# First norm's modulation weights from the second quarter on: halves in working tiles, with priorities that fall by quarter

## The chip, the cores and the metric

The kernel runs on one core of one Trainium2 chip. The metric is the device time of one execution in microseconds (us): the median of several runs, smaller is better. Beside it stands one profiled execution, from which every row of a view below is taken. TensorE (PE) multiplies matrices, VectorE (DVE), ScalarE (ACT) and GpSimd (POOL) work elementwise, SyncE (SP) issues the DMA transfers. Each engine works through its own instructions in a fixed order and waits where an operand or a buffer isn't ready.

## The reference

Four transformer layers in a row on one sequence of 256 tokens (plus 256 context tokens in the first one), 1024 channels, all in float32. Every norm of every layer is modulated by vectors that are computed from a conditioning vector `c`; this is the part that the change touches. Cut to what matters:

```python
# first_block, layer 0 (even mixer) and layer 1 (odd mixer)
ml = split(silu(c)     @ ada_w[layer] + ada_b[layer], 6)   # 1024 -> 6*1024, for the 256 latent tokens
mc = split(silu(c_ctx) @ ada_w[layer] + ada_b[layer], 6)   # the same for the 256 context tokens
a_lat = rms_norm(h_lat, norm1_w) * (1 + ml[1]) + ml[0]
a_ctx = rms_norm(h_ctx, norm1_w) * (1 + mc[1]) + mc[0]
o_lat, o_ctx = mixer(a_lat, a_ctx, ...)                    # layer 0: a_lat @ w_in (1024 x 2240), attention + GLA
h_lat = h_lat + ml[2] * o_lat
h_lat = h_lat + ml[5] * mlp(rms_norm(h_lat, norm2_w) * (1 + ml[4]) + ml[3])
# second_block, two hybrid layers of the same form on the result, with weights w_mod (1024 -> 6*1024) and SwiGLU
```

The modulation weights of one layer are 1024 x 6144 float32, 25 MB, used for one or two vectors only.

## The kernel before, in words

**Planning.** The program first records all its operations in program order, without issuing them. A planner then simulates the five engines with a list of costs and writes out the order of each engine by hand. Among the operations that are ready and whose tiles have a free slot, an engine takes the one with the smallest key `(index - early) * 200 - path`, where the index is the operation's place in program order, `early` is a bonus in places that the code sets, and `path` is the planner's cost in ns from there to the end. The SP queue of transfers is ordered in the same way; a load goes out as soon as SP is free, its tile's slot is free, and nothing with a smaller key can go. A transfer that was recorded while `nc.behind` was set isn't issued before the operation of that index. The order written out is fixed: on the chip an engine waits for the operation that is next in it.

**Tiles.** A tag has a fixed number of slots: raw mixer weights `wraw` 4 of 128 x 1024 (512 KB), their split high and low parts `whi`, `wlo` 3 each, raw modulation weights `mraw` 4 of 512 KB (`MODRAW`), working tiles of 128 x 512 (tag `t512`) 47 (`H2`), PSUM banks `ps` 6 and one for the modulation banks (`modps`). Each weight piece is split into a high and a low part (`whi` on ACT or DVE, `wlo` on DVE), and a block of a product is three matmuls: `xnh` with `whi`, `xnh` with `wlo`, `xnl` with `whi`.

**The start of layer 0.** `layer0` needs scale (j = 1) and shift (j = 0) of the first norm. Their weights are stored by quarters: quarter q of j holds the 256 output channels 256q to 256q+255, and its 1 MB is two pieces (h = 0, 1) of 512 KB, one for each half of the input channels. `mod_quarter` loads the two pieces into two `mraw` tiles, multiplies them on PE into one PSUM bank `modq` (16 matmuls that are recorded with `nc.together()`, so that they stay in one run), copies the bank out (`modqs`), transposes it (`modqt`) and adds the bias (two DVE operations on `mod`). After the two vectors of a quarter, `a1` is ready for channel blocks 2q and 2q+1; with it and `rstd`, `norm_mod` makes `ny` and its parts `xnh`, `xnl` of these two blocks. All quarters are recorded with `early` = `EARLYQ` - q * `STEPQ`, with 1500 and 0, so 1500 for all. After quarter 0 (`BEHIND` = 0), `nc.behind` is set to the last load recorded so far, so everything loaded later goes behind quarter 0.

**Around it.** Program order: `x` (eight loads of 256 KB, 2 KB per partition) at indices 14 to 21, the quarters at 36 to 95, the norm's square sums (`sq`, `ss`, `rstd`) and `ny` up to 155, the 18 pieces of the first projection (`ein`) between 156 and 690, the modulation bank of j = 2 (8 pieces through `mod_bank`, `early` 1500) at 1539, those of j = 4, 3, 5 from 1795 on, also with 1500. Each group of `ein` needs all eight blocks of `xnh`, `xnl`; with three pieces split and six PSUM banks, several groups can be partly summed before the last blocks are there. Where PE would sit idle for long, the planner puts dummy matmuls (`filled`), which keep its clock up and compute nothing that is used.

Of the kernel before, what the change touches and what calls it, by code (L numbers as in the profile page):

```python
# [11 lines left out]
F32 = mybir.dt.float32  # L12
# [742 lines left out]
class Kernel:  # L755
    RAW, HI, MODRAW, MODRUN = 4, 3, 4, 2
    LEAD = (5, 2, 1)
    EARLYQ, STEPQ, BEHIND = 1500, 0, 0
    CV, CQ = range(6), ()
    PINP = range(4)  # L760
    EARLY = (1500, 1000, 500, 300)
# [114 lines left out]
    def mod_quarter(self, j, q, dest, bias):  # L876

        nc = self.nc
        ps = self.ps("modq")
        nc.early = self.EARLYQ - q * self.STEPQ  # L880
        raws = [nc.tile(self.mp, [128, 1024], F32, "mraw", "mraw", self.MODRAW) for _ in range(2)]
        for h in range(2):
            nc.sync.dma_start(raws[h], self.A["mod0"][j * 8 + q * 2 + h])
        with nc.together():
            for k in range(4):
                for g in range(4):
                    h, t = g // 2, g % 2
                    self.mm(ps[32 * g:32 * g + 32, 0:128], self.cst[:, 0, h * 4 + k, :],
                            raws[h][:, k * 256 + t * 128:k * 256 + t * 128 + 128], k == 0, k == 3)
        sb = self.t([128, 128], "modqs")  # L890
        nc.scalar.activation(sb, ps[:, 0:128], AF.Copy)
        pt = self.ps("modqt")
        nc.tensor.transpose(pt[:, 0:128], sb, self.c_ident)
        c = slice(j * 8 + q * 2, j * 8 + q * 2 + 2)
        src = pt[:, 0:128].rearrange("p (h t r) -> p h t r", h=2, t=2)
        nc.vector.tensor_tensor(dest[:, c, :], src[:, 0, :, 0:2], bias[:, c].unsqueeze(2).to_broadcast([128, 2, 2]), op=ALU.add)
        nc.vector.tensor_tensor(dest[:, c, :], src[:, 1, :, 0:2], dest[:, c, :], op=ALU.add)
        nc.early = 0
# [1293 lines left out]
```

## Time and profile before

| | |
|---|---|
| median of 3 runs | 1997.41 us (1995.1 to 2007.69) |
| the profiled execution's own time | 1992.15 us |
| its span, first to last instruction | 1990.4 us |
| PE busy | 1915.1 us, 96% of the span |
| DVE, ACT, POOL busy | 1375.8, 891.7, 220.0 us |
| bytes moved | 328.14 MB, mean 165 GB/s |
| mean granted TensorE clock | 0.989 |

PE is busy nearly all the time, but "busy" holds dummy matmuls and matmuls whose modelled ends overlap. What a change at the start is worth is read from the first 62 us: how much of PE's time there is work that is used, and what the rest waits for.

### The profile page before, as it was taken

To read this page: it belongs to the slowest core of one execution; us is meant where nothing else is said; L and a number is where in the kernel's file an instruction comes from. 1 tells how busy PE (TensorE), PEld (TensorE's weight loads), DVE (VectorE), ACT (ScalarE), POOL (GpSimd) and SP (SyncE) were. 2 spreads that over 40 slices of the span, in tenths; PEclk is the share of its full clock that TensorE was granted. 3 is DMA by queue.
4 is the path that set the end of the run, shared out by engine and by line. 5 is a ranking of instruction groups with operands and counts; after the bars stand their busy time and mean duration, and the time that the engine had idled before them with its cause. 6 is when DMAs were issued, how large, how long until landed. Compare 5 with 4: busy or idle time off the path is not lost.

```text
span 1990.4 us, 37698 instructions
## 1 busy us (share of the span) xinstructions
PE 1915.1 (96%) x15067; PEld 1611.4 (81%) x15067; DVE 1375.8 (69%) x2934; ACT 891.7 (45%) x1880; POOL 220.0 (11%) x214
## 2 busy tenths in 40 slices
PE   7999999999999999889999999999999999989998
PEld 5766657888888877677899997877999978679998
DVE  5436777555546468875678777898877689878773
ACT  4125464321212165533355336675654265656541
POOL 1001002000000042013011003200300031012000
PEclk9998999999999999989999999999999999999999
DMA  9683306242323237577437556455555765445651
GB/s 335 211 290 117 117 12 204 62 130 90 118 74 115 77 123 191 181 215 222 127 107 237 187 194 223 155 188 193 177 181 185 250 211 181 148 160 170 184 196 56
DMA packets 108444, 328.14 MB, mean 165 GB/s; under 512 B 27211, under 2 KB 28491, under 8 KB 108140
## 3 DMA queue, kind: packets, MB, share of 16 engines
q1 hardware_dynamic: 108268, 325.73, 50.7%
q8 instruction: 118, 1.93, 0.4%
q14 instruction: 58, 0.48, 0.1%
HBM read 320.45 MB, written 5.24 MB: 164 GB/s over the span
## 4 chain that ended last, share of the span: by engine, by line
PE 80%; DVE 8%; DMA 7%; ACT 3%; issue 2%; POOL 0%; SPq 0%; DVEq 0%; ACTq 0%; POOLq 0%
PE ps L708 62%; PE modps L708 3%; DMA mraw<-in_mod_dram 2%; DMA wraw<-in_hin_dram 2%; PE filled L708 1%; PE sc L708 1%; DVE wlo L708 1%; PE ss L708 1%; DMA wraw<-in_hout_dram 1%; DMA wraw<-in_oin_dram 1%; DVE dlo L708 1%; DVE invt L708 1%; DVE inv L708 1%; PE gdno L708 1%; PE po L708 1%
## 5 line engine op out<-in xcount | busy, mean ns | idle before, releaser
L708 ACT ACTIVATE dhi<-wraw 128x512 fp32r<-128x512 f32 x397 | 237.7, 624 | 264.0 <-PE ps L708 132.4
L708 DVE TENSOR_TENSOR dlo<-wraw,dhi 128x512 fp32r<-128x512 f32 x456 | 305.5, 697 | 69.3 <-PE ps L708 53.6
L708 PE MATMUL ps<-xnh,dhi 128*128 128x256 f32 (+1 forms) x920 | 248.2, 304 | 3.9 <-ACT xnh L708 2.4
L708 PE MATMUL ps<-xnh,dlo 128*128 128x256 f32 (+1 forms) x920 | 248.8, 305 | 1.1 <-DVE dlo L708 1.1
L708 PE MATMUL ps<-xnl,dhi 128*128 128x256 f32 (+1 forms) x920 | 248.3, 304 | 0.1
L708 PE MATMUL ps<-xnh,whi 128*128 128x256 f32 (+1 forms) x776 | 232.6, 331 | 9.8 <-DVE ogg L708 5.7
L708 DVE TENSOR_TENSOR wlo<-wraw,whi 128x512 fp32r<-128x512 f32 x340 | 232.4, 711 | 13.1 <-ACT whi L708 9.2
L708 PE MATMUL ps<-xnh,wlo 128*128 128x256 f32 (+1 forms) x776 | 231.9, 331 | 3.2 <-DVE wlo L708 3.2
L708 PE MATMUL ps<-xnl,whi 128*128 128x256 f32 (+1 forms) x776 | 231.8, 331 | 0.8 <-DVE xnl L708 0.8
L708 PEld LDWEIGHTS ps<-xnh,dhi 128*128 128x128 f32 x920 | 165.4, 191 | 13.5 <-ACT xnh L708 2.9
L708 PEld LDWEIGHTS ps<-xnh,dlo 128*128 128x128 f32 x920 | 165.4, 191 | 10.4 <-DVE dlo L708 1.8
L708 PEld LDWEIGHTS ps<-xnl,dhi 128*128 128x128 f32 x920 | 165.5, 191 | 8.0 <-DVE xnl L708 0.7
L708 DVE CAST whi<-wraw 128x1024 fp32r<-128x1024 f32 x82 | 56.8, 693 | 158.4 <-PE ps L708 133.8
L708 PEld LDWEIGHTS ps<-xnh,whi 128*128 128x128 f32 x776 | 143.7, 193 | 27.7 <-issue 6.2
L708 PEld LDWEIGHTS ps<-xnh,wlo 128*128 128x128 f32 x776 | 144.1, 193 | 21.3 <-DVE wlo L708 4.8
L708 PEld LDWEIGHTS ps<-xnl,whi 128*128 128x128 f32 x776 | 143.7, 193 | 17.1 <-issue 4.6
L708 ACT ACTIVATE whi<-wraw 128x1024 fp32r<-128x1024 f32 x88 | 92.9, 1056 | 102.2 <-PE ps L708 58.4
L708 PE MATMUL ps<-mh,dhi 128*128 128x512 f32 (+1 forms) x336 | 105.9, 336 | 0.1
L708 PE MATMUL ps<-mh,dlo 128*128 128x512 f32 (+1 forms) x336 | 105.9, 336 | 0.0
L708 PE MATMUL ps<-ml,dhi 128*128 128x512 f32 (+1 forms) x336 | 105.8, 336 | 0.0
L708 PE MATMUL modps<-mraw,cst 128*32 128x256 f32 x1408 | 97.7, 393 | 5.8 <-DMA mraw<-in_mod_dram 4.9
L708 POOL TENSOR_TENSOR ny<-x,rstd 128x256 f32<-128x256 f32 (+1 forms) x45 | 50.1, 1140 | 414.8 <-ACT rstd L708 414.8
(558 smaller groups left out, 4114.4 us busy)
## 6 DMA issues: line engine op xcount, KB each, us to landing
mraw<-in_mod_dram SPq DMA_DIRECT2D x192, 512.0 KB
wraw<-in_mlp_dram SPq DMA_DIRECT2D x128, 512.0 KB
wraw<-in_gu_dram SPq DMA_DIRECT2D x88, 512.0 KB
wraw<-in_hin_dram SPq DMA_DIRECT2D x54, 512.0 KB
wraw<-in_dn_dram SPq DMA_DIRECT2D x44, 512.0 KB
wraw<-in_oin_dram SPq DMA_DIRECT2D x25, 512.0 KB
wraw<-in_ein_dram SPq DMA_DIRECT2D x18, 512.0 KB
wraw<-in_hout_dram SPq DMA_DIRECT2D x16, 512.0 KB
```

The costliest lines, as they stand in the source:

```text
L708: getattr(self.real[op.eng], method)(*a, **kw)
```

## The change

Three edits. `STEPQ` becomes 750, so `early` is 1500, 750, 0 and -750 for quarters 0 to 3. The pieces of quarters 1 to 3 no longer go into `mraw` tiles: each 512 KB piece is loaded by two transfers of 256 KB into two working tiles of 128 x 512 named `mrawq` (2 KB per partition and transfer in place of 4 KB). The matmuls are the same, and read the half that holds their columns. Quarter 0 stays as it was. The 12 loads of quarters 1 to 3 become 24, and the operations behind them move up by 12 in program order.

```diff
-    EARLYQ, STEPQ, BEHIND = 1500, 0, 0
+    EARLYQ, STEPQ, BEHIND = 1500, 750, 0
...
         nc.early = self.EARLYQ - q * self.STEPQ
-        raws = [nc.tile(self.mp, [128, 1024], F32, "mraw", "mraw", self.MODRAW) for _ in range(2)]
+        raws = []
         for h in range(2):
-            nc.sync.dma_start(raws[h], self.A["mod0"][j * 8 + q * 2 + h])
+            w = self.A["mod0"][j * 8 + q * 2 + h]
+            if q < 1:
+                raw = nc.tile(self.mp, [128, 1024], F32, "mraw", "mraw", self.MODRAW)
+                nc.sync.dma_start(raw, w)
+                raws.append([raw[:, 0:512], raw[:, 512:1024]])
+            else:
+
+                raws.append([self.t([128, 512], "mrawq") for _ in range(2)])
+                for c in range(2):
+                    nc.sync.dma_start(raws[h][c], w[:, c * 512:c * 512 + 512])
         with nc.together():
...
-                            raws[h][:, k * 256 + t * 128:k * 256 + t * 128 + 128], k == 0, k == 3)
+                            raws[h][k // 2][:, k % 2 * 256 + t * 128:k % 2 * 256 + t * 128 + 128], k == 0, k == 3)
```

## Rows read from the trace of the kernel before

**Rows 1.** The page's head and the busy time of each engine

```profile
span 1990.4 us, 37698 instructions
...
PE 1915.1 (96%) x15067; PEld 1611.4 (81%) x15067; DVE 1375.8 (69%) x2934; ACT 891.7 (45%) x1880; POOL 220.0 (11%) x214
```

**Rows 2.** Windows: length, busy by engine (x instructions), granted clock, DMA share, GB/s

```profile
0.00:27.70 27.70, 16.40 (x118) 10.56 (x118) 16.53 (x40) 15.39 (x27) 2.66 (x6) 1.00 0.94 351
27.70:51.94 24.24, 22.47 (x243) 15.89 (x244) 13.78 (x29) 10.06 (x22) 5.66 (x4) 1.00 0.88 316
51.94:62.04 10.10, 9.90 (x74) 5.29 (x73) 6.84 (x14) 3.16 (x6) 0.00 (x0) 1.00 0.90 322
62.04:127.90 65.86, 65.86 (x390) 48.38 (x389) 23.88 (x41) 10.14 (x18) 0.00 (x0) 1.00 0.66 231
```

**Rows 3.** The same windows for the dummy matmuls alone (PE, PEld)

```profile
27.70:51.94 24.24, 1.56 (x5) 0.86 (x5) 1.00 0.88 316
```

**Rows 4.** Windows by the transfers' stages, columns as in Rows 2

```profile
0.00:15.00 15.00, 7.36 (x72) 5.15 (x73) 3.91 (x12) 5.87 (x12) 0.20 (x4) 1.00 0.87 308
9.00:15.00 6.00, 4.62 (x36) 3.39 (x37) 2.50 (x6) 3.65 (x7) 0.00 (x0) 1.00 1.03 366
15.00:35.00 20.00, 15.88 (x105) 10.69 (x104) 19.79 (x38) 14.06 (x25) 8.12 (x5) 1.00 1.03 403
35.00:40.00 5.00, 5.00 (x78) 3.62 (x76) 1.18 (x4) 0.52 (x2) 0.00 (x0) 1.00 0.55 172
```

**Rows 5.** Waits of SP's queue in 0 to 62: total us, times, longest

```profile
SPq L708 <- PE modq L708: 14.2, 6, 3.1
```

**Rows 6.** Timeline of SP: start, length, transfer, count

```profile
3.07 1.02 SPq L708 DMA_DIRECT2D x<-in_xT_dram  x2
...
7.59 3.74 SPq L708 DMA_DIRECT2D x<-in_xT_dram  x4
...
37.58 0.80 SPq L708 DMA_DIRECT2D mraw<-in_mod_dram  x2
```

**Rows 7.** Timeline of PE, its weight loads and DVE around the first norm

```profile
19.23 2.08 PE L708 MATMUL ss<-sq,cst 128*128 128x512 f32 x2 [2.75 <-DVE sq L708]
...
27.73 0.98 PE L708 MATMUL ps<-xnh,whi 128*128 128x512 f32 x3 [0.94 <-ACT xnh L708]
...
29.44 0.81 PEld L708 LDWEIGHTS modq<-mraw,cst 128*32 128x32 f32 x32 [0.36 <-issue]
29.45 1.08 PE L708 MATMUL modq<-mraw,cst 128*32 128x128 f32 x32
...
46.31 1.08 PE L708 MATMUL modq<-mraw,cst 128*32 128x128 f32 x32
...
51.25 0.69 DVE L708 TENSOR_TENSOR xnl<-ny,xnh 128x512 fp32r<-128x512 f32 x1
```

**Rows 8.** Timeline of ACT around the first norm

```profile
14.46 2.72 ACT L708 ACTIVATE sq<-x 128x512 f32<-128x512 f32 x4 [0.41 <-DMA x<-in_xT_dram]
...
20.76 1.04 ACT L708 ACTIVATE whi<-wraw 128x1024 fp32r<-128x1024 f32 x1
...
24.54 0.63 ACT L708 ACTIVATE rstd<-rstd 128x512 f32<-128x512 f32 x1
```

**Rows 9.** The chain that ended last, in order of time

```profile
62.04 31.77 PE ps L708 x140
...
127.91 7.54 DMA mraw<-in_mod_dram
```

**Rows 10.** Timeline: first instruction of each hybrid layer (ACT), last addition (DVE)

```profile
1216.91 1.31 ACT L708 ACTIVATE lead<-x,ha 128x256 fp32r<-128x256 f32 x3 [0.55 <-DVE x L708]
...
1597.23 0.91 ACT L708 ACTIVATE lead<-x,ha 128x256 fp32r<-128x256 f32 x2 [1.28 <-DVE x L708]
...
1986.72 0.75 DVE L708 TENSOR_TENSOR x<-x,fy 128x256 f32<-128x256 f32 x2
```

**Rows 11.** A window with a lower granted clock, columns as in Rows 2

```profile
160.00:180.00 20.00, 20.00 (x84) 12.13 (x82) 10.75 (x14) 12.84 (x25) 3.35 (x3) 0.74 0.32 105
```

## The prediction

> **What bounds the kernel now.** I read the page's head first [rows 1]: PE is busy for 96% of the span, so a gain has to come from PE time that isn't used, and it is worth what PE can then do earlier. The change touches only the first norm, so I cut the start into windows [rows 2]. From 62.04 to 127.9 PE is busy for 65.86 of 65.86 us: from there on it has work in hand, and whatever the start saves up to 62.04 is carried on. Before the first used projection matmul (27.73 [rows 7]) PE does almost nothing that counts. Between 27.73 and 62.04, that is in 34.3 us, it idles 24.24 - 22.47 = 1.8 and 10.10 - 9.90 = 0.2 us, and 1.6 us are dummy matmuls [rows 2, 3]. So 30.8 us of it are real work. This is the first thing to see: the wait for the last quarters is mostly covered already, by partly summed projection groups.
>
> Next the transfers [rows 4]: 403 GB/s from 15 to 35 us, then only 172 between 35 and 40. SP's waits say why [rows 5]: 14.2 us in which the next load was held because its tile still waited for a modq run on PE. The two loads at 37.58 [rows 6], in the middle of the dip, are of this kind: the modq run that frees their tiles stands in PE's fixed order behind projection matmuls. The last modq run starts at 46.31 and the last block of xnl ends at 51.94 [rows 7].
>
> **The change, part by part.**
>
> *Order of the transfers.* By the keys, quarter 1 (bonus 750) now goes ahead of x, cst, pos and vec (bonus 0, about 40 places earlier); quarter 2 (bonus 0) follows them; quarter 3 (-750) comes behind everything that is recorded within some 750 places behind it and has a free slot. That is not much: four ein pieces (wraw has 4 slots) and four tiles of the j = 2 bank (mraw has 4, free after quarter 0). SP needs about 0.5 us per issue [rows 6], far less than the transfer takes, so in the plan all slots are taken before the first comes free, and quarter 3 is next. In MB, from the shapes: quarter 0 2.10, quarter 1 2.10, x and small constants 2.88, quarter 2 2.10, gup and the first ein piece 0.59, mraw 2.10, three ein pieces 1.57, cst1 0.26, quarter 3 2.10: 15.8 in all. None of these has to wait for a slot on the chip, so SP's 14.2 us of waiting go, and the 12 additional issues (12 x 0.5 = 6 us of SP) lie beside the transfers; without that cover they would cost up to 6 us.
>
> *When they land.* The window to 15 us moved 15 x 308 = 4.62 MB, after that 403 GB/s. Rate of the halves: the nearest rows are the stretch from 9 to 15, mostly x, whose loads have the same shape (366), and 403. Quarter 2 ends at 9.2 MB: 15 + 4.6/0.403 = 26.3 us. Quarter 3 ends at 15.8 MB: 15 + 11.2/0.403 = 42.7; with 6.3 MB at 366 it is 1.6 us later, 44.3. I take 43. Its two modq runs cost PE 2 x (1.08 + 0.36) = 2.9 us [rows 7], and the last xnl ends 5.6 us after the start of the last run, as now (51.94 - 46.31): about 50, and 2 earlier if PE takes the runs at once. So the last blocks come 2 to 4 us earlier.
>
> *What moves off the PE path.* Three modq runs (the second of quarter 1, both of quarter 2) can now run before the first projection matmul, where PE has only dummies: 3 x 1.44 = 4.3 us, with their transposes about 5.3. Matmuls, copies and additions are the same in number, shape and cost.
>
> *What it costs.* x lands 2.10/0.386 = 5.4 us later, at 20.5 us instead of about 15 (0.386 is between the two rates above). Now the last square ends at 17.2 and rstd at 25.17 [rows 8]: 8.0 us, of which only an addition, the ss matmuls (2.08) and two activations (0.63 each) follow from each other, about 4. So rstd is at 25.2 to 29.1, against 25.17, and the first projection matmul, 2.56 us behind it, at 27.8 to 31.7. The first ein piece lands at 27.8 (9.8 MB) and needs 1.04 us for its high part [rows 8] and some 0.7 for the first half of the low one: 29.5. I take 30, so 2.3 us later than now.
>
> *Sum.* Real work left from 30 on: 30.8 - 5.3 = 25.5 us. Idle and dummies: between 0 and today's 3.5, and I take 2, as the supply is close: until xnl is complete three split pieces give 54 matmuls of 31.77/140 = 0.227 us [rows 9], 12.3 us, plus two bank runs and two modq runs of 1.44 us, 18 us for the 18 to 20 us between 30 and 48 to 50. So the state of 62.04 is reached at 30 + 25.5 + 2 = 57.5: **4.5 us** saved, with bounds of 1.3 (31.7 and 3.5) and 8.7 (27.8 and 0). The profiled execution's own time is 1992.15; by this it becomes 1987.6. It lies 5.3 us below the median of the runs, so I take the saving off the median: 1997.4 - 4.5 = 1992.9. The clock doesn't enter: it is granted in full in all windows up to 127.9 [rows 2].
>
> *A rule that speaks against it.* The eight loads of x, of the same shape as the halves, moved at 366 GB/s, 9% below the larger pieces [rows 4], which is the 1.6 us above. The Trainium skill, DMA: Bandwidth & Descriptors (Rules for kernel authors), asks for at least 1 MiB per DMA for full bandwidth, and fits 2.0 us plus bytes over 436 GB/s to one DMA of another issuing path; if each DMA paid that by itself, 24 halves would be an estimated 24 x 2.6 = 62 us where 12 pieces are 12 x 3.2 = 38, so 24 us would be lost. The trace doesn't agree for transfers in a queue: 512 KB pieces reach 403 GB/s, far above what that fit gives one of them.
>
> **The rivals.**
>
> *A. Given back (or never had).* The chain waits for a bank tile at 127.91, 7.54 us long [rows 9]. If the banks of j = 4, 3, 5 land no earlier than now, PE arrives there 4.5 us earlier and waits. Or rstd takes its 8 us and the start gives up what the quarters bring. Against: PE is fully busy up to that point, and the j = 2 bank's first tiles now go out before quarter 3, so the banks are ahead too. Time: 1997.4.
>
> *B. Quarter 3 starves: slower.* Its bonus of -750 puts it behind all four banks by key. If in the plan the mraw tiles come free before SP gets to quarter 3, further tiles pass it: 2.10 MB for each set of four, 5.2 us. The first set is covered by the supply above; from the second on PE runs dry. All of them are 14.7 MB, 36.5 us; less the 14 bank runs that PE does in that time (14 x 1.44 = 20) and 3 of slack, 13 us lost: 2010. Against: tiles come free only when transfers land, and SP is by then long past.
>
> *C. Halves are slow.* The four x loads at 7.59 took 3.74 us, 0.94 each [rows 6], because SP waited for landings. At that pace, not 0.65 (256 KB at 403 GB/s), 24 halves cost 7 us: 1997.4 - 4.5 + 7 = 2000. Against: the whole stretch around these loads moved 366 GB/s. By the estimate from the Trainium skill above (DMA: Bandwidth & Descriptors) it would be some 2017; I leave that inside this rival's chance.
>
> *D. Another order downstream.* The planner's order of everything later shifts. The two hybrid layers run the same program in different orders: 1597.23 - 1216.91 = 380.3 and 1986.72 + 0.75 - 1597.23 = 390.2 us [rows 10], so order alone is worth up to 10 us a layer. A stretch at clock 0.74 for 20 us [rows 11] is worth 20 x 0.26 = 5 us more or less. Time: 1983 or 2003.
>
> **How the numbers follow.** Forecast (a saving of 1.3 to 8.7): 0.60, the time 1992.9. A 0.17, B 0.06, C 0.05, D 0.12, half each way. The range reaches 10 + 5 us (D's two terms) on either side of the forecast and a little more below for its upper bound of 8.7: 1977 to 2007; it holds A, C and most of D, and leaves out B and the tails. A change of 1%, 20 us, is about what a measurement of this kernel can tell from none, as its three runs lie 12.6 us apart. Faster by over 1% would take the forecast and a lucky order in more than one layer, 0.06; slower by over 1% needs B at its worst with an unlucky order, 0.05; within it 0.89.
>
> **What would show it.** Right: SP's waits for PE modq nearly gone in the first 62 us; the DMA near 400 GB/s up to about 43 us without the dip at 35 to 40; x after quarter 1, with the square sums ending some 4 us later; four modq runs of quarters 1 and 2 before the first projection matmul at 29 to 31; the last modq run at 43 to 45; the projection matmuls and bank runs that are done at 62.04 now, done at about 57.5. Wrong: the last modq run behind 52 (B), mrawq transfers below 300 GB/s (C), a longer chain wait near 125 (A), or equal starts and a difference that grows from 300 us on (D).

## The result and the profile after

The changed kernel takes 2004.39 us (median of 20 runs, 1995.25 to 2018.53) against 1993.18 for 20 runs of the kernel before beside it: ratio 1.0059, 95% interval 1.004 to 1.0078. It is slower by 0.6%, 11 to 12 us, where 4.5 us less were forecast. (The forecast of 1992.9 us was taken off the median of 3 runs, 1997.41, which lies 4.2 us above that of 20.) The profiled execution took 1998.07 us, with a span of 1996.3.

The same stretches as in [rows 2], and the transfers as in [rows 4]:

```profile
0.00:27.70 27.70, 13.15 (x141) 8.00 (x141) 9.80 (x34) 10.95 (x21) 0.20 (x4) 0.81 0.96 346
27.70:51.94 24.24, 20.84 (x148) 13.65 (x148) 14.77 (x22) 14.02 (x25) 7.57 (x5) 0.79 1.03 402
51.94:62.04 10.10, 9.95 (x122) 6.40 (x120) 1.43 (x8) 0.44 (x2) 0.00 (x0) 1.00 0.67 228
...
35.00:40.00 5.00, 2.71 (x16) 1.34 (x20) 4.49 (x5) 5.00 (x11) 2.65 (x2) 0.79 1.03 395
40.00:50.00 10.00, 9.84 (x43) 6.91 (x36) 5.93 (x10) 4.40 (x7) 0.00 (x0) 0.76 1.04 401
```

The transfers do what was forecast: 402 GB/s in place of 316 in the second stretch, and the dip at 35 to 40 us is gone (395 in place of 172). But PE is busy for 20.84 us there in place of 22.47, and the granted clock, 1.00 before, is 0.81 and 0.79. Waits of SP's queue in 0 to 62 (as [rows 5]), and its timeline (as [rows 6]):

```profile
SPq L708 <- PE modps L708: 8.5, 3, 6.1
SPq L708 <- DMA mrawq<-in_mod_dram: 6.5, 20, 0.5
...
9.59 1.00 SPq L708 DMA_DIRECT2D x<-in_xT_dram  x2
10.94 0.33 SPq L708 DMA_DIRECT2D cst<-in_cst_dram  x1
...
13.67 2.37 SPq L708 DMA_DIRECT2D x<-in_xT_dram  x4
...
24.52 0.35 SPq L708 DMA_DIRECT2D wraw<-in_ein_dram  x1
...
28.90 1.77 SPq L708 DMA_DIRECT2D wraw<-in_ein_dram  x3
31.63 8.70 SPq L708 DMA_DIRECT2D mrawq<-in_mod_dram  x8
```

The waits for modq runs, 14.2 us before, are gone. x is issued from 9.59 to 16.0 where it began at 3.07, and quarter 3 goes out from 31.63 to 40.33. The first pieces of the projection, `wraw`, are issued at 24.52 and from 28.90 on. PE's timeline, as [rows 7]:

```profile
18.16 1.09 PE L708 MATMUL modqt<-cst,modqs 128*128 128x128 f32 x4 [3.18 <-DMA cst<-in_cst_dram]
18.90 3.33 PE L708 MATMUL filled<-fill 128*128 128x512 f32 x7
26.05 2.04 PE L708 MATMUL ss<-sq,cst 128*128 128x512 f32 x2 [3.81 <-DVE sq L708]
28.02 1.94 PE L708 MATMUL modq<-mrawq,cst 128*32 128x128 f32 x32
...
36.05 0.51 PE L708 MATMUL ps<-xnh,whi 128*128 128x512 f32 x1 [1.19 <-ACT xnh L708]
...
40.84 2.50 PE L708 MATMUL filled<-fill 128*128 128x512 f32 x5
43.50 0.80 PE L708 MATMUL ps<-xnh,whi 128*128 128x512 f32 x1 [0.16 <-ACT whi L708]
...
58.79 1.96 PE L708 MATMUL modq<-mrawq,cst 128*32 128x128 f32 x64
...
61.24 0.93 PE L708 MATMUL filled<-fill 128*128 128x512 f32 x3
```

Read it from top to bottom: the sums `ss` start at 26.05 (19.23 before), the first projection matmul at 36.05 (27.73), and until 43.50 PE has little but dummies and a bank between single matmuls; from there on they follow each other. The two runs of quarter 3 (one row, x64) stand at 58.79 (the last one at 46.31 before), though their loads had all been issued by 40.33. ACT between the two (as [rows 8]):

```profile
20.46 2.66 ACT L708 ACTIVATE sq<-x 128x512 f32<-128x512 f32 x4 [0.41 <-DMA x<-in_xT_dram]
...
29.38 0.63 ACT L708 ACTIVATE rstd<-rstd 128x512 f32<-128x512 f32 x1
32.05 0.28 ACT L708 ACTIVATE modqs<-modq 128x128 f32<-128x128 f32 x1 [2.05 <-PE modq L708]
32.23 1.05 ACT L708 ACTIVATE whi<-wraw 128x1024 fp32r<-128x1024 f32 x1
...
42.40 1.99 ACT L708 ACTIVATE whi<-wraw 128x1024 fp32r<-128x1024 f32 x2
```

The last square ends at 23.1 and rstd at 30.0. ACT then waits 2.05 us for quarter 2's run on PE and splits the first piece before it takes up the first norm; the second and third pieces are split only at 42.40, behind all blocks of the norm that are ready. DVE, in the changed kernel:

```profile
25.22 0.68 DVE L708 TENSOR_TENSOR sq<-sq 128x512 f32<-128x512 f32 x1
...
42.99 0.68 DVE L708 TENSOR_TENSOR wlo<-wraw,whi 128x512 fp32r<-128x512 f32 x1
```

And SP and DVE in the kernel before:

```profile
14.45 1.69 SPq L708 DMA_DIRECT2D wraw<-in_ein_dram  x3
...
23.89 1.29 DVE L708 TENSOR_TENSOR wlo<-wraw,whi 128x512 fp32r<-128x512 f32 x2
```

Before, four pieces were issued by 16.1 us, and three of them were split by 25.2, while ACT and DVE had to wait for rstd anyway. In the changed kernel quarters 1 and 2 go ahead of them, DVE makes the first low part at 42.99, and their splitting falls into the time in which ACT and DVE make the first norm.

**A mark for the start.** The last copy `cq` out of PSUM in the first stage comes, in every kernel here, when all four modulation banks and 376 or 378 matmuls into the banks `ps` are done, nearly the whole first projection. (Some expectations use an earlier mark, the first `kpe` matmul, at 57.7 us before and 68.8 after the change; it stands at different places in PE's order, in e3 at 57.74 with `cq` 3.0 us late, so `cq` is the better one.) ACT's timeline, before and after:

```profile
146.74 0.60 ACT L708 ACTIVATE cq<-ps 128x512 f32<-128x512 f32 x1 [5.45 <-PE ps L708]
```

```profile
152.74 0.60 ACT L708 ACTIVATE cq<-ps 128x512 f32<-128x512 f32 x1 [3.86 <-PE ps L708]
```

So the start loses 6.0 us up to there. The table puts all kernels beside each other (us; one profiled execution each; "last run" is the start of the last row with a modq run, which holds both runs of quarter 3 in the changed kernel, e1, e2, e5 and e11):

| kernel | ss | first projection matmul | last run | last cq copy | ratio to before (95%) |
|---|---|---|---|---|---|
| before | 19.23 | 27.73 | 46.31 | 146.7 | 1 |
| changed | 26.05 | 36.05 | 58.79 | 152.7 (+6.0) | 1.0059 (1.004 to 1.0078) |
| e1 constants first | 26.00 | 36.01 | 58.47 | 153.0 (+6.3) | 1.0048 (1.0017 to 1.0079) |
| e2 x first | 18.89 | 32.22 | 52.06 | 147.8 (+1.0) | 1.0045 (1.002 to 1.007) |
| e3 falling loads only | 27.05 | 34.15 | 47.78 | 149.7 (+3.0) | 1.0153 (1.0115 to 1.0191) |
| e4 both | 18.69 | 31.66 | 46.24 | 145.1 (-1.6) | 1.0054 (1.0027 to 1.0081) |
| e5 changed start, order of before behind it | 25.98 | 35.98 | 58.44 | 152.8 (+6.1) | 1.0062 (1.0032 to 1.0092) |
| e6 start of e4, order of before behind it | 18.75 | 32.69 | 46.64 | 146.1 (-0.7) | 0.9993 (0.9966 to 1.002) |
| e7 before, order a | 18.91 | 27.42 | 46.33 | 145.7 (-1.0) | 1.0022 (0.9992 to 1.0052) |
| e8 before, order b | 19.31 | 27.83 | 46.27 | 146.2 (-0.5) | 1.0076 (1.0048 to 1.0104) |
| e9 halves only | 36.03 | 45.90 | 25.81 | 155.0 (+8.2) | 1.0133 (1.0086 to 1.0181) |
| e10 falling bonus only | 18.90 | 27.42 | 54.41 | 151.8 (+5.1) | 1.0174 (1.0138 to 1.021) |
| e11 x first, halves | 19.00 | 39.69 | 35.99 | 147.8 (+1.1) | 0.9969 (0.9941 to 0.9997) |
| e12 x, bias first, halves | 19.06 | 37.21 | 34.32 | 146.1 (-0.7) | 0.9997 (0.9973 to 1.002) |
| e13 start of e12, order of before behind it | 19.07 | 37.85 | 34.96 | 146.1 (-0.6) | 1.0003 (0.9978 to 1.0028) |

### The profile page after: what moved, and what is told of

It reads as the page before. It is cut to its first block, busy times and chain, and to the rows that moved or that the text cites. A ratio compares the mean times of both kernels' runs of the same rounds, so it can differ in the third digit from the quotient of the medians.

```text
span 1996.3 us, 37728 instructions
## 1 busy us (share of the span) xinstructions
PE 1918.5 (96%) x15079; PEld 1614.0 (81%) x15079; DVE 1372.7 (69%) x2944; ACT 892.7 (45%) x1880; POOL 216.9 (11%) x204
## 4 chain that ended last, share of the span: by engine, by line
PE 81%; DVE 7%; DMA 4%; ACT 2%; issue 1%; SPq 1%; POOL 0%; DVEq 0%; ACTq 0%; POOLq 0%
PE ps L708 64%; PE modps L708 3%; PE filled L708 1%; SPq L708 1%; PE sc L708 1%; DMA wraw<-in_oin_dram 1%; PE ss L708 1%; DVE invt L708 1%; DMA mraw<-in_mod_dram 1%; DVE dlo L708 1%; PE gdno L708 1%; DVE inv L708 1%; PE po L708 1%; PE glao L708 1%; DVE fy L708 1%
## 5 line engine op out<-in xcount | busy, mean ns | idle before, releaser
L708 DVE CAST whi<-wraw 128x1024 fp32r<-128x1024 f32 x75 | 52.5, 700 | 151.9 <-PE ps L708 122.6
L708 ACT ACTIVATE whi<-wraw 128x1024 fp32r<-128x1024 f32 x95 | 100.2, 1056 | 97.9 <-PE ps L708 47.3
```

Source lines behind the costliest of these rows:

```text
L708: getattr(self.real[op.eng], method)(*a, **kw)
```

## The experiments

**e1, constants first.** `cst`, from which the dummies' operand is made, goes ahead of quarter 1: does the clock matter?

```diff
+            nc.early = 1000
             self.load_consts(0, keep=True)
+            nc.early = 0
```

> The changed kernel with one edit: the first constants (cst0, 0.39 MB, which the dummy matmuls, the transposes and the ss matmuls need) get a bonus of 1000, so that they go out right behind quarter 0 and ahead of quarter 1. The order of PE is otherwise that of the changed kernel in all but its first 25 lines, so downstream order can't explain a difference. Theory 'clock' (cst0 lands at 18 instead of 12, so the dummies start at 18.9, PE is idle from 15 on, the granted clock falls to 0.50 to 0.79 between 15 and 45 us, and everything on PE there takes up to twice as long): granted clock 1.00 from 15 to 45, first projection matmul at 34 to 35 instead of 36.05, 2 to 6 us faster than the changed kernel, ratio to before 1.003 to 1.005. Theory 'x late' or 'late PE runs' alone: the clock is back, but the first projection matmul stays at 36 and the last modq run at 57 to 59, ratio 1.005 to 1.007, as the changed kernel's 1.0059.

Windows of this kernel, 5 us each (the changed kernel was granted 0.74, 0.50, 0.50 in the last three):

```profile
10.00:15.00 5.00, 5.00 (x44) 3.49 (x40) 0.29 (x1) 0.69 (x2) 0.00 (x0) 1.00 1.05 388
15.00:20.00 5.00, 3.99 (x64) 3.21 (x57) 2.69 (x6) 2.58 (x5) 0.00 (x0) 1.00 1.05 383
20.00:25.00 5.00, 1.00 (x5) 0.50 (x3) 4.00 (x19) 3.80 (x5) 0.00 (x0) 1.00 1.05 385
25.00:30.00 5.00, 3.91 (x34) 1.86 (x34) 1.80 (x6) 3.56 (x6) 0.00 (x0) 0.51 1.05 389
```

With dummies from 11 us on the clock holds to 25 us and then falls to 0.51, behind 5.0 us in which PE waits for the square sums. Nothing else moved: 36.01 and +6.3. The part of the clock that was mended is not what costs; the part after 25 us was not tried. The ratio of 1.0048 lies in the band of the theory 'clock', but its interval, 1.0017 to 1.0079, also holds the changed kernel's 1.0059, so it doesn't tell the two apart.

**e2, x first.** `x`, `pos` and `cst` get a bonus of 1000, so they go ahead of quarter 1.

```diff
+                nc.early = 1000
                 nc.sync.dma_start(xk, self.A["xT"][:, k, :])
+                nc.early = 0
```

> The changed kernel with cst0, pos and the eight loads of x given a bonus of 1000: they go out behind quarter 0 and ahead of quarter 1, the rest of the change stays. Theory 'x late' (the 2.1 MB of quarter 1 ahead of x push the square sums, rstd and the first projection matmul back by 7 to 8 us): ss at 19 to 21 as before, rstd by 25, first projection matmul at 29 to 31 (it waits for the first ein piece, which lands at 28), granted clock 1.00; start mark kpe (before 57.7, changed 68.8) at 60 to 63, ratio 0.999 to 1.003. Theory 'late PE runs' alone: the quarter 3 runs still stand behind the partial sums, last modq run at 53 or later, kpe at 64 or later, ratio 1.003 to 1.006.

`ss` is back at 18.89 and the mark moves by 5.0 us, from +6.0 to +1.0. The last runs still stand behind partial sums, at 52.06. The edit moves `cst` too, which by itself gave nothing back in e1, and the granted clock is higher as well (1.00 from 40 to 45 us, 0.53 in the changed kernel), so the 5.0 us hold whatever the clock cost there. Two things were missed. The first projection matmul comes at 32.22, not by 31: rstd ends at 23.4 and the first `xnh` at 26.5, but PE waits for the first split piece, which ACT makes only at 31.12. And the ratio is 1.0045 where at most 1.003 was expected.

**e3, falling bonus for loads only,** and **e4**, e2 and e3 together. Behind the loads of a quarter its work gets 1500 again:

```diff
                     nc.sync.dma_start(raws[h][c], w[:, c * 512:c * 512 + 512])
+        nc.early = self.EARLYQ
```

> The changed kernel, but the falling bonus holds for the loads alone: the matmuls, copies and additions of a quarter keep 1500. Theory 'late PE runs' (quarter 3's bonus of -750 is given to its modq runs too, which the planner therefore puts on PE behind 46 projection matmuls and two bank runs, at 58.8, although their weights landed by about 43): the last modq run moves to 46 to 50, xnl complete at 52 to 56 instead of 65.4, kpe at 61 to 64, ratio 1.002 to 1.004. Theory 'x late' alone: PE has 54 projection matmuls to do in between anyway, so only the bubble of 3 us behind the late run goes; kpe at 65 or later, ratio 1.004 to 1.006.

> Both edits: x, cst0 and pos ahead of quarter 1, and the falling bonus for the loads alone. This is the change as the prediction understood it, with its worst cost taken out. If 'x late' and 'late PE runs' are together the cause: first projection matmul at 29 to 31, last modq run at 43 to 47, granted clock 1.00, kpe at or before 57.7, ratio 0.996 to 1.000. If it is slower than 1.003 with such a start, the rest of the loss lies in the order downstream.

The runs of quarter 3 come at 45.07 and 47.78 in e3, and the mark moves by 3.0. Together the two edits move it by 7.6, nearly the sum of 5.0 and 3.0. So the loss at the mark has two sources, and they are told apart: x behind quarter 1 (with the clock that comes with it), and the late runs. The times don't follow. e4 is at 1.0054 with a mark 1.6 us ahead of the kernel before, where 0.996 to 1.000 was expected; by the condition that was written down its loss lies in the order downstream. e3 is 1.5% slower because layer 1 (first convolution copy to first instruction of the hybrid layers) takes 523.5 us there and 497.8 before, in a program that is the same but for its order.

**e5 and e6, starts with the order of before behind them.** The planner's order of the kernel before is kept from its own time of 450 us on. On the chip the last instruction of ACT and DVE that stands elsewhere than in the kernel before comes at about 350 us in e5 and 410 in e6; the start and the rest of layer 0's mixer keep the new order. The edit is in the planner alone:

```diff
+        for i, e in after:
+            op = self.idle[0] if i < 0 else ops[i]
+            op.eng = e
+            order.append(op)
         return order
```

> The start of the changed kernel with the downstream order of the kernel before: the planner first plans the kernel before; everything that it starts before its 450 us is then planned again with the change, and what comes later is issued in the old order (the last 10010 of 11452 PE instructions are the same as before). Theory 'start': the changed start alone is worth +7 us at the beginning of layer 1 (first conv output at 726 instead of 719), and stays so to the end: span 1996 to 1999, ratio 1.002 to 1.005. Theory 'downstream order' (the loss comes from the reordered layers): ratio 0.999 to 1.001.

> The start with x, cst0 and pos ahead of quarter 1 and falling bonuses for the loads alone, and the downstream order of the kernel before (the last 9620 of 11437 PE instructions are the same). In the run with the same start and the planner's own order, layer 1 began 3.9 us earlier than before and the end came 10.8 us later. Theory 'start and order are separate': layer 1 begins 2 to 5 us earlier and the end does too, span 1984 to 1989, ratio 0.996 to 1.000. If the gain of the start is given back by waits downstream whatever the order: ratio 1.000 to 1.003.

e5 is 1.0062, as the whole change and a little more than the theory's 1.005: the order behind 350 us isn't needed to explain the loss. It doesn't speak of the order between the mark and 350 us, which is the changed kernel's in e5. e6 is 0.9993: with both sources taken away nothing is left of the loss, and nothing is gained that can be measured. Its layer 1 was expected 2 to 5 us earlier than before and begins 3.0 us later (722.1, 719.1 before), so the 0.7 us at the mark are not carried on.

**e7 and e8, order alone.** The kernel before with one cost of the planner changed, `LOADED = 950` to 960 and to 940; the start is the same to within 0.4 us.

> The kernel before with nothing of the change; the planner's cost of a landed transfer (LOADED) is 960 instead of 950 ns. Its order on PE is the same as before up to instruction 374, behind all projections of layer 0, and differs in some 4500 lines after it. Theory 'downstream order is worth several us either way': start the same (kpe at 57.7), the end 5 to 20 us away from before in one direction. Theory 'order hardly matters': ratio 0.998 to 1.002.

> The same with LOADED 940: another downstream order, the start the same as before up to instruction 270 of PE. Expectations as for the one with 960: 5 to 20 us away in one direction if order is worth so much, 0.998 to 1.002 if not. Together with the other the two give the spread that a change of order alone makes, against which the changed kernel's 1.0059 has to be read.

1.0022, an interval that holds 1, and 1.0076: the second loses 15 us with a mark 0.5 us earlier. An order that nobody chose can be worth as much as the change.

**e9, halves only,** and **e10, falling bonus only.**

```diff
-    EARLYQ, STEPQ, BEHIND = 1500, 750, 0
+    EARLYQ, STEPQ, BEHIND = 1500, 0, 0
```

> The halves in working tiles alone, with one bonus (1500) for all four quarters. The transfers then go out as quarter 0, the 24 halves, x, the rest, so x is behind 8.4 MB. Theory (what counts is when x comes, since nothing of the projection can start before rstd): at 0.39 MB/us x is complete at about 29, the ss matmuls start at 33 to 36, the first projection matmul at 42 to 45, all quarters' runs before it. PE then has nothing to wait for, but starts 15 us later than the kernel before with about 9 us less to do (six quarter runs and their transposes): the last cq copy 3 to 8 us later than in the kernel before (146.7), so at 150 to 155, and the time 1.002 to 1.009 of it, more or less by what the order downstream does. Rival (the late last quarter is what costs, x is covered): the last quarter's run is early here, so the last cq copy is at 144 to 147 and the ratio at 0.995 to 1.001.

With 8.4 MB ahead of x the last run is done by 27.7, some 20 us sooner than before, and the mark is 8.2 us late. That is just outside the 3 to 8 that was written down, and far from the rival's. The time, 1.0133 in 4 runs, is beyond the 1.009 of the theory.

```diff
-            if q < 1:
...
-                raws.append([self.t([128, 512], "mrawq") for _ in range(2)])
+        raws = [nc.tile(self.mp, [128, 1024], F32, "mraw", "mraw", self.MODRAW) for _ in range(2)]
```

> The falling bonus alone, all quarters in the raw modulation tiles as in the kernel before. x goes out as before (quarter 1 waits for quarter 0's tiles anyway). Theory (the bonus that also holds for the quarter's own work on PE makes the last blocks late, and x makes the start late, each by itself): the ss matmuls at 19 to 20 and the first projection matmul at 27 to 29 as before; quarter 3's loads behind tiles of the j = 2 bank, its run on PE at 52 to 62 (46.31 before) and the first kpe matmul at 59 to 68 (57.7 before); the last cq copy 1 to 5 us later than before, 148 to 152. Rival (only the late x costs): the last cq copy within 1 us of 146.7. The time is 1.000 to 1.006, and says less, as the order downstream is another one.

The edit is shown against the changed kernel; against the kernel before it is `STEPQ` alone. x is on time (`ss` at 18.90, first projection matmul at 27.42), the mark is still 5.1 us late. SP's waits and PE's timeline:

```profile
SPq L708 <- PE modq L708: 15.7, 6, 4.8
...
53.23 0.41 PE L708 MATMUL modq<-mraw,cst 128*32 128x128 f32 x4 [2.70 <-DMA mraw<-in_mod_dram]
54.41 1.07 PE L708 MATMUL modq<-mraw,cst 128*32 128x128 f32 x28 [0.78 <-DMA mraw<-in_mod_dram]
```

Here it isn't PE's order but the queue: quarter 3 waits for four slots behind tiles of the j = 2 bank, and PE waits for it. This is rival B, in the kernel without the working tiles; the halves are what removes it. Most of the 1.7% (4 runs; 1.000 to 1.006 was expected) comes later: the hybrid layers start at 1244.6, 27.7 us late, of which 5.1 stand at the mark.

**e11 to e13, quarters 1 to 3 as halves with one bonus behind x.** e11:

```diff
-        nc.early = self.EARLYQ - q * self.STEPQ
+        nc.early = self.EARLYQ if q < 1 else 750
...
+                nc.early = 1000
                 nc.sync.dma_start(xk, self.A["xT"][:, k, :])
+                nc.early = 0
```

> Quarter 0, then x and the constants (bonus 1000), then quarters 1 to 3 as halves in working tiles with one bonus of 750 for loads and work. Theory: the ss matmuls at 18 to 20 and the first projection matmul at 31 to 33 as in the other kernels with x ahead, all quarters' runs by about 40 and xnl complete at 44 to 48, so the last cq copy at 143 to 146 (146.7 before, 145.1 with x ahead and falling loads): a start 1 to 3 us ahead of the kernel before, the time 0.998 to 1.005, as the order downstream decides the rest. Rival (the first projection matmul alone decides, at 31 to 33 in place of 27.73): the last cq copy at 148 to 151.

The start is not what was expected: 39.69 and +1.1. PE and DVE show why:

```profile
35.62 0.45 PE L708 MATMUL modqt<-cst,modqs 128*128 128x128 f32 x1 [5.00 <-DVE mod L708]
...
35.11 0.23 DVE L708 TENSOR_TENSOR mod<-modqt,vec 128x4 f32<-128x4 f32 x2 [5.22 <-DMA vec<-in_vec_dram]
```

The bias vector `vec`, a quarter of a megabyte, was left behind the 24 halves, and everything stands for it. The time is 0.9969 all the same. e12 puts `vec` ahead, e13 is e12's start with the order of before behind it, as e5.

> As the kernel with x ahead and all halves at 750, and the bias vector (vec) ahead of the halves as well: behind them it came so late that DVE waited 5.2 us for it (to 35.1) before it could finish the first norm's scale. Theory (the start is worth what it shows at the end of the first stage): the first projection matmul then waits for its own first weight piece, behind 11.9 MB, so at 34 to 37 in place of 39.7, xnl is complete by 41 to 44, and the last cq copy comes 1 to 4 us ahead of the 147.8 there, at 143.5 to 147; the time 0.992 to 1.000 of the kernel before, as the order downstream is another one. Rival (after the first norm PE works through the same supply of split weight pieces whatever comes first): the last cq copy stays at 147 to 149.

> The start of the kernel with x, constants and bias ahead of the halves, with the planner's order of the kernel before from its time 450 us on. Theory (the start decides): the ratio follows the last cq copy, 1 us for 1 us or somewhat more, so 0.994 to 0.9995 with a copy at 143.5 to 147. Rival (what the kernel with x ahead and halves at 750 gained, 0.9969, came from its order downstream): 0.9985 to 1.003 here.

```profile
37.21 0.47 PE L708 MATMUL ps<-xnh,whi 128*128 128x512 f32 x1 [0.58 <-DVE whi L708]
```

That is e12: xnl is complete at 41.6, ten us ahead of the kernel before, and from 37.21 on the projection matmuls follow each other; yet the mark is 0.7 us early, and both times are 1.0 to within 0.3%. What is won on the last blocks is paid by the first matmul, which now waits for its own weights behind 12 MB. e11's 0.3% is thus not put down to its start, as its mark is 1.8 us behind e12's; that it comes from the order downstream is argued and not shown. e13 lies in the band that was written down for its rival and just outside that of the theory, but 0.6 us at the mark are 0.03% of the time: too little to tell whether the time follows it.

## Why the prediction was wrong, point by point

- **Right: the transfers.** Order, the vanished waits, the rate (395 to 402 GB/s), quarter 3 in the low forties, SP's additional issues hidden. Rival C is refuted by the rate. Rival B is refuted for the change as it is (e10 shows that it would have come without the halves): its sign, a last modq run behind 52, came at 58.79, but from PE's order and not from starved loads. Of rival A, the part on rstd is in what follows; the wait for a bank tile isn't, as PE is busy for 87.5 of the 88 us from 62 to 150.
- **Wrong: "I take 30, so 2.3 us later than now".** Measured 36.05, 8.3 later and 4.3 beyond the bound of 31.7. rstd ends 4.8 us later, at 30.0, 0.9 beyond the upper bound of that term. The bound doesn't come out of the rows: with x 5.4 us later the last square would end at 17.2 + 5.4 = 22.6 (measured 23.1), and 4 to 8 us behind it is 26.6 to 30.6, not 25.2 to 29.1. Of the 8.0 us, 6.9 remained and not about 4: DVE's fixed order makes the last addition of the squares only at 25.22. The rest lies between rstd and the first matmul: 6.0 us in place of the 2.56 that were carried over from the row of before. ACT's rows above show 2.05 us of waiting for a modq run and 0.94 of splitting in between: the runs that were "moved off the PE path" into the gap put their copies into ACT's fixed order ahead of the first norm. e2 puts x (with the constants) back ahead and gives back 5.0 us at the mark; its first matmul, at 32.22, then waits for the split of its weights, which the prediction had at 29.5.
- **Wrong: "the last xnl ends ... about 50, and 2 earlier if PE takes the runs at once".** It was costed from the landing alone. `early` belongs to every operation of the quarter, so -750 also puts its runs on PE behind partial sums and banks: 58.79, and the last xnl at 65.4. The code says so: `nc.early` is set ahead of the quarter's loads and matmuls alike. e3 gives the work its 1500 back and wins 3.0 us.
- **Mis-sized: "idle and dummies ... I take 2".** Between 36.05 and 43.50 PE waits for split pieces that ACT makes only at 42.40, and after the late runs it has three dummies and 0.48 us of waiting. By the forecast's own sum 36.05 + 25.5 + idle = 62.04 + 6.0, so idle, dummies and slow clock are 6.5 us in place of 2; the trace has 2.0 us of idle time and 4.1 of dummies from 36.05 to 68.04. The supply of 18 us was counted in pieces that have landed, not in pieces that ACT and DVE have had time to split.
- **Wrong: "the clock doesn't enter".** It fell to 0.50, because PE's cover, the dummies, hangs on a constant that the change moves behind quarter 1. What it cost is not settled: e1 mends it up to 25 us and moves nothing.
- **Rival D was real and given too little.** e7 and e8 alone differ by 0.5%; e3, e9, e10 lose more than their starts. The order behind 350 us isn't the cause of the change's loss, as e5 shows; the order in the rest of layer 0's mixer is not ruled out. The wide range (1977 to 2007) comes from this rival; that the measured 2004.39 lies in it is luck and no support for the mechanism.
- **The saving itself wasn't there.** With x first and the quarters' work no longer late (e6, e13) the time is that of before within 0.3%; the 4.5 us were not confirmed, and 0.6 to 0.7 us at the mark is what the traces show. The first projection matmul stays late in both (32.69 and 37.85), as its weights come behind the quarters.

Still open: 6.0 us stand at the mark, 11 to 12 in the medians. A second place is the rest of layer 0's mixer. The first addition to x at its end, in the kernel before, the changed one, e1 and e5:

```profile
301.55 0.87 DVE L708 SCALAR_TENSOR_TENSOR x<-ps,mod,x 128x256 f32<-128x256 f32 x2
```

```profile
309.30 0.87 DVE L708 SCALAR_TENSOR_TENSOR x<-ps,mod,x 128x256 f32<-128x256 f32 x2
```

```profile
312.73 0.87 DVE L708 SCALAR_TENSOR_TENSOR x<-ps,mod,x 128x256 f32<-128x256 f32 x2
```

```profile
312.53 0.87 DVE L740 SCALAR_TENSOR_TENSOR x<-ps,mod,x 128x256 f32<-128x256 f32 x2
```

The changed kernel is 7.8 us late there and e5, with the same order up to there, 11.0. The clock accounts for the difference. From 160 to 180 us PE is busy throughout, and the profiled execution of the kernel before was granted 0.74 [rows 11], the changed one and e5:

```profile
160.00:180.00 20.00, 20.00 (x113) 13.05 (x112) 14.27 (x20) 13.63 (x26) 2.76 (x3) 1.00 0.45 154
```

```profile
160.00:180.00 20.00, 20.00 (x94) 12.14 (x94) 11.91 (x17) 10.71 (x20) 1.29 (x1) 0.83 0.29 89
```

(e1 was granted 0.83 as well.) By 20 us times what is missing from 1.00, these dips cost an estimated 5.2, 0 and 3.4 us. Without them the changed kernel, e1 and e5 are all some 13 us behind the kernel before. By then they have done three runs of modulation matmuls more (416 matmuls in place of 368), some 3 us that are moved and not lost. So by this estimate some 10 us are lost up to there: 6 at the mark and 4 in the rest of the mixer, where the order of the changed kernel stands in e5 too. What loses these 4 isn't shown. In e5 little is added behind it: it is 9.0 us late at the first hybrid layer and 12.3 at the end.

## What to carry to other kernels

A priority that a code region sets holds for everything recorded in it: before you move a load by it, list the matmuls, copies and additions that move too, and look where each fixed engine order puts them. Cost the first use of a stage from all that it needs (activations, the split weights, the small constants and the engine that prepares them), and don't carry over the distance between two instructions from a trace in which other work lay between them. Where PE is busy throughout behind the start, earlier last blocks are worth nothing if they are paid with a later first matmul; pick one mark behind which all variants have done the same work, and compare there.

## What the runs showed of the hardware

- Transfers of 256 KB in one queue moved 395 GB/s from 35 to 40 us, where they are quarter 3's halves, nearly as much as the larger pieces (403 [rows 4]). The Trainium skill, DMA: Bandwidth & Descriptors (Rules for kernel authors), asks for 1 MiB or more for full bandwidth; this trace doesn't agree for loads that follow each other.
- The granted clock fell to 0.50, its level of 1.2 GHz, at about 17.5 us, in a PE gap of 3.18 us, and was 0.50 from 20 to 30 us, through another gap of 3.81; a quarter's matmuls that take 1.08 us [rows 7] took 1.94. The Trainium skill, TensorE: Matmul & The Clock Gate (Why this matters for your kernels), tells to keep gaps out from between bursts of matmuls; by that rule, the trace agrees.
- Runs of one kernel follow the mean granted clock: 28 of 29 runs of the kernel before beside e1 to e4 reach from 1978.29 us at 0.996 to 2000.95 at 0.983, some 1.7 us for 0.001. So a median of many runs is needed for less than 1%, and two single profiles are compared with their clocks beside them: the dip at 160 to 180 us was 0.74 in one and 1.00 in the other.
